# Thirty-two experts worked on in twelve units instead of thirteen

## The chip, the cores and the metric

One core of one Trainium2 chip runs the whole layer in one launch. The metric is device time in microseconds (us): 880.14 us before, the median of 3 runs (879.83 to 881.45). The engines are named as in the profile: PE (TensorE, with its weight loads as PEld), DVE (VectorE), ACT (ScalarE), POOL (GpSimd) and SP (SyncE, which issues all loads).

## The reference, cut to what matters

The layer mixes 512 tokens of width 1024 by pooling and attention, normalises, and then sends every token to 2 of 32 experts. An expert is three matrices of 2 MB each, so all experts together are 32 x 6 MB of weights that are read once from memory.

```python
group_probs = jax.nn.softmax(xf @ w_rg + b_rg, axis=-1)
g_idx = jnp.argmax(group_probs, axis=-1)                     # one of 4 groups
expert_logits = jnp.einsum('td,gde->tge', xf, w_re) + b_re   # 8 experts in a group
...
top_vals, top_idx = lax.top_k(sel_logits, TOP_K_IN_GROUP)    # two of the eight
...
for g in range(N_GROUPS):
    for e in range(EXPERTS_PER_GROUP):
        h = jax.nn.silu(xt @ w_eg[g, e]) * (xt @ w_eu[g, e])
        y = y + (h @ w_ed[g, e]) * combine[:, g, e, None]
...
ple = jax.nn.sigmoid(x @ w_pg[i]) * (p[i] @ w_pp[i])
x = layer_norm(DEEPNORM_ALPHA * x + moe_out + ple, ln2_g[i], ln2_b[i])
```

## The kernel before, in words

Up to about 370 us the kernel does the mixers, the first normalisation and the routing. From there on it works on the experts in **units**. A unit fills the 128 columns of PE with slots for tokens: a unit of kind `p` has two experts with 64 slots each, a unit of kind `q` four experts with 32 slots each. `KINDS = "ppppqqqpppppp"` lists the thirteen units 0 to 12. The first `FIXED` experts are taken by number, the others by rank, that is in order of how many tokens they got: the `BIG` largest get 64 slots (`CAP`), the rest 32. Ranks are known only when the counts are (`rank`), so until then only fixed experts can be loaded. If an expert had more tokens than slots, a branch at the end of the program would work on all experts again.

For each unit, `pair(j, ...)` does this on PE: `inner` (gate and up matrices, n = 0 and 1, eight k-steps each, all experts of the unit side by side as column parts of PE), the scatter of the unit before (`scatter_steps`), the turn of `h` (`hT_ps`), and `outer` (the down matrix, f = 0 to 3). In every second unit it also gathers the tokens of the next two units into slots (`gather`, 64 matmuls in two halves behind f = 1 and f = 3; a buffer `xg` for each unit, 2 of them). Before the change the odd units gather; the slots of units 0 and 1 are gathered during the routing. Units 3 to 6 (`EMB`) also carry the last term of the layer (`embedding`, `pg_ps`), in 26 steps.

Weights come in **pieces** of 1 MB (1.05 million bytes), 6 for each expert, 192 in all. SP issues them in one queue, in the order in which `load_chunk` is called. `eload_first` brings 18 pieces during the earlier stages; two of these lie in rooms (`acc`) that can't be used again, so 16 rooms circulate. `eload_past` runs behind every fourth k-step and every second f: it hands the rooms of the pieces just used to the next pieces. `KEEP` takes up to 8 rooms away from units 2 to 6 for the embedding; they come back at unit 7. In the last unit the last two pieces come as four halves, by columns.

The program's tail behind the last `outer` sums each block of tokens on PE, normalises and stores.

Of the kernel before, what the change touches and what calls it, by code (L numbers as in the profile page):

```python
# [21 lines left out]
NT = S // 128  # L22
# [4 lines left out]
LAG = 3  # L27


FIXED, BIG, CAP = 4, 16, 64  # L30
KINDS = "ppppqqqpppppp"
ALPHA = 2.0 ** 0.25
EPS = 1e-5

# [2 lines left out]
def layer_kernel(ctx: ExitStack, tc: tile.TileContext, x, p, w_in, w_pool, pool_scale, w_pu, w_au,  # L37
                 w_o, ln1_g, ln1_b, w_rg, b_rg, w_re, b_re, w_eg, w_eu, w_ed, w_pg, w_pp,
                 ln2_g, ln2_b, out):
    nc = tc.nc  # L40
# [37 lines left out]
    iota_c = cst.tile([128, CAP], F32, name="iota_c")  # L78
# [311 lines left out]
    units = [(h, tb) for h in range(HEADS) for tb in range(NT)]  # L390
    f = fill()
# [14 lines left out]
    for half in range(2):  # L406
        for br, (w, ah, al) in enumerate(((wpu, poh, pol), (wau, aoh, aol))):
            hi, lo = wnext()
            for c in range(4):
                g = gates[2 * br + half][:, c]  # L410
# [3 lines left out]
                o = mm()  # L414
# [17 lines left out]
    x1, acc = {}, {}  # L432
# [37 lines left out]
    units, chunk0, elist = [], [], []  # L470
    n_fixed, n_big, n_small = 0, 0, BIG
    for kind in KINDS:
        n = 2 if kind == "p" else 4
        if n_fixed < FIXED:
            who, n_fixed = (False, n_fixed), n_fixed + n
        elif n == 2:
            who, n_big = (True, n_big), n_big + n
        else:
            who, n_small = (True, n_small), n_small + n
        units.append(who + (n,))  # L480
        chunk0.append(len(elist))
        es = [(len(units) - 1, i) for i in range(n)]
        elist += [(w, e, slice(4 * kk, 4 * kk + 4), 4, FE) for w in (weg, weu) for kk in range(2) for e in es]
        elist += [(wed, e, slice(2 * kk, 2 * kk + 2), 2, D) for kk in range(2) for e in es]
    NU = len(units)
    assert n_fixed == FIXED and n_big == BIG and n_small == E - FIXED
    numbers = {}

    def expert(u, i):

        by_rank, first, _ = units[u]
        if not by_rank:
            return first + i
        if (u, i) not in numbers:
            r = first + i
            numbers[u, i] = nc.values_load(order[0:1, r:r + 1], engines=(mybir.EngineType.SP,), min_val=0, max_val=E - 1,
                                           skip_runtime_bounds_check_because="an expert's number")
        return numbers[u, i]

    def source(i):  # L500
# [2 lines left out]


    FIRST = [(0, "s8"), (1, "s8"), (2, "s8"), (4, "s8"), (5, "wraw"), (6, "whi"), (8, "wlo"), (9, "wraw"), (10, "s8"),
             (11, "s8"), (12, "s8"), (13, "s8"), (14, "whi"), (15, "wlo"), (3, "acc"), (16, "more"), (17, "more"),
             (7, "acc")]
    ew = {}

    room_of = {}  # L510

    def load_chunk(i, tag):
        room_of[i] = tag
        a, b = elist[i][3:]
# [20 lines left out]
    def eload_past(n):  # L535

        while done[0] < n:
            tag = room_of[done[0]]
            done[0] += 1
            if tag == "s8" and kept[0] < keep[0]:  # L540
                kept[0] += 1
            elif tag != "acc":
                free.append(tag)
        while free and len(ew) < len(elist):
            load_chunk(len(ew), free.pop(0))

    def give_back():

# [257 lines left out]
    xgs = {}  # L806

    def slots_and_weights(u):
        by_rank, first, n = units[u]
        return [t[:, :, first:first + n] for t in ((ranked[False], ranked[True]) if by_rank else (posm, comb))]  # L810

    def one_hots(G, m, b):

        for i in range(G.shape[2]):
            pos, _ = slots_and_weights(2 * m + i)
            n = pos.shape[2]
            shape = [128, 2, n, 128 // n]
            nc.vector.tensor_tensor(G[:, :, i].rearrange("p b (e c) -> p b e c", e=n),
                                    iota_c[:, None, None, :128 // n].to_broadcast(shape),
                                    pos[:, b:b + 2, :, None].to_broadcast(shape), op=OP.is_equal)  # L820

    def gather(G, o, kb, tbs):

# [13 lines left out]
        nc.tensor.matmul(o, strict[:, :1].to_broadcast([128, 128]), strict[:, None].to_broadcast([128, 4, 128]),  # L837
                         start=True, stop=False)

    def slots_of(m):  # L840
        for j in range(2 * m, min(2 * m + 2, NU)):
            xgs[j] = slp.tile([128, KD, 128], F32, name="xg", bufs=2)

    def keep_slots(m, o, kb):
        o = o.rearrange("p (k e s) -> p k e s", k=2, e=2)
        ks = slice(2 * kb, 2 * kb + 2)
        nc.scalar.activation(xgs[2 * m][:, ks], o[:, :, 0], AF.Copy)
        if 2 * m + 1 < NU:
            nc.vector.tensor_copy(xgs[2 * m + 1][:, ks], o[:, :, 1])

    def weights_of(j):

        pos, com = slots_and_weights(j)
        n = pos.shape[2]
        shape = [128, NT, n, 128 // n]

        if j < NU - 1:
            Gw = ex.tile([128, NT, 128], F32, name="Gw", tag="yh", bufs=2)
        else:
            Gw = outs[1][:, 0, :512].rearrange("p (b s) -> p b s", b=NT)  # L860
        G4 = Gw.rearrange("p b (e c) -> p b e c", e=n)
        nc.vector.tensor_tensor(G4, iota_c[:, None, None, :128 // n].to_broadcast(shape),
                                pos[:, :, :, None].to_broadcast(shape), op=OP.is_equal)
        nc.vector.tensor_mul(G4, G4, com[:, :, :, None].to_broadcast(shape))
# [19 lines left out]
    def inner(j, n, o, ks):  # L884


        ne = units[j][2]
        c = 128 // ne
        for k in ks:
            for i in range(ne):  # L890
                nc.tensor.matmul(o[i * c:(i + 1) * c], xgs[j][:, k, i * c:(i + 1) * c],  # L891
                                 ew[chunk0[j] + ne * (2 * n + k // 4) + i][:, k % 4], start=k == 0, stop=k == KD - 1)
            if k % 4 == 3:
                eload_past(chunk0[j] + ne * (2 * n + k // 4 + 1))

    with tc.manual_schedule():
        G = [lnt.tile([128, 2, 2, 128], F32R, name="G")]
        dve, pool = nc.vector, nc.gpsimd
        out_proj(0, 1, o, parts)
        eload_first(9)  # L900
# [50 lines left out]
        affine(2, 1, pool)  # L951
        normalise(3)
        place(0)
        one_hots(G[0], 0, 0)
        gain(2, 0, dve)
        xs = [mm("xg_ps") for _ in range(4)]
        for o in xs:
# [22 lines left out]
        eload_first(18)  # L980
        place(2)
        gather(G, xs[3], 3, (0, 1))
        G.append(lnt.tile([128, 2, 2, 128], F32R, name="G", tag="wr2"))
        one_hots(G[1], 0, 2)
        counted = count_tokens()
        slots_of(0)
        for kb in range(4):
            gather(G, xs[kb], kb, (2, 3))
            keep_slots(0, xs[kb], kb)
            if kb == 1:  # L990
                first = mm()
# [11 lines left out]
    def pair(j, other, extra):  # L1003


        last = j == NU - 1
        m = (j + 1) // 2 if j % 2 and j + 1 < NU else None

        def embed(i):
            for _ in range(extra[i]):  # L1010
# [2 lines left out]

        h = ex.tile([128, FE], F32, name="h", bufs=1)

        four = units[j][2] == 4

        def scatter():
            if other:
# [36 lines left out]
            scatter()  # L1056
            scatter()
        if m:
            G = [ex.tile([128, 2, min(2, NU - 2 * m), 128], F32R, name="G", tag="yl", bufs=2) for _ in range(2)]
            for b in range(2):  # L1060
                one_hots(G[b], m, 2 * b)
            slots_of(m)
# [17 lines left out]
        for f in range(4):  # L1080
            for c in range(2):
                outer(j, hT, f, c, o[c])
            if f % 2:
                eload_past(chunk0[j] + units[j][2] * (4 + (f + 1) // 2))
            if m and f % 2:
                og = [zz("xg_ps") for _ in range(2)]
                for i in range(2):
                    gather(G, og[i], f - 1 + i, range(NT))
                    keep_slots(m, og[i], f - 1 + i)
            if f == 1:  # L1090
                embed(4)
                Gt, ws = turn_one_hots(Gw)
# [1 line left out]
        return Gt, [weighted(o[c], ws) for c in range(2)]  # L1094

    def outer(j, hT, f, c, o):
        ne = units[j][2]
        n = 128 // ne
        for i in range(ne):
            nc.tensor.matmul(o[i * n:(i + 1) * n], hT[:, f, i * n:(i + 1) * n],  # L1100
                             ew[chunk0[j] + ne * (4 + f // 2) + i][:, f % 2, halves[c]], start=f == 0, stop=f == 3)

    def weighted(o, ws):
# [267 lines left out]
```

## Time and profile before

| what | value |
|---|---|
| median of 3 runs | 880.14 us |
| the profiled execution | 882.05 us, its span 880.3 us |
| PE busy | 824.1 us (94%) |
| DMA queue of the loads, share of 16 engines | 70.6% |
| mean granted TensorE clock | 0.972 |

The profile's span runs from the first instruction to the last; the execution's own time is 1.75 us longer. A busy PE counts overlapping matmuls once, so a share of 94% says that PE was rarely without work, not which resource set the pace.

### The profile page before, as it was taken

The numbers are of one execution on the slowest core, as the hardware profiler recorded it, in microseconds if no ns is written. First come the engines' busy times: TensorE is split into PE (matmuls) and PEld (weight loads), VectorE is DVE, ScalarE is ACT, GpSimd is POOL, SyncE is SP. The second block draws the span as 40 slices with busy tenths as digits, with TensorE's granted clock in tenths as the row PEclk, the third lists the DMA queues.
The fourth block names the chain that finished last, engine by engine and source line by source line (L and its number), as shares of the span: only waits on it lengthen the run. The fifth ranks groups of instructions, "written<-read, shape, count | busy, mean of one in ns | idle before, by whom it ended". The sixth has DMA issues, their size and how long they took to land.

```text
span 880.3 us, 11414 instructions
## 1 busy us (share of the span) xinstructions
PE 824.1 (94%) x4382; PEld 524.5 (60%) x4382; DVE 421.6 (48%) x705; ACT 216.8 (25%) x447; POOL 192.1 (22%) x176
## 2 busy tenths in 40 slices
PE   8999899899999998899999977989899999999993
PEld 7886677677768886734545522656765544644542
DVE  5278647554558758775244331222131424442347
ACT  3123444453551115212100211202010011010134
POOL 3333324233322227300002202211230000000045
PEclk9999999999999999699999989999999999999997
DMA  7431131312115796489999799999999999999962
GB/s 251 141 98 49 48 96 48 96 48 96 48 49 190 199 392 240 181 312 408 406 421 385 282 418 417 410 407 383 385 386 418 420 419 420 418 420 420 420 243 98
DMA packets 65786, 241.87 MB, mean 275 GB/s; under 512 B 12096, under 2 KB 32576, under 8 KB 41408
## 3 DMA queue, kind: packets, MB, share of 16 engines
q1 hardware_dynamic: 65728, 241.10, 70.6%
q8 instruction: 36, 0.59, 0.3%
q14 instruction: 22, 0.18, 0.1%
HBM read 238.99 MB, written 2.10 MB: 274 GB/s over the span
## 4 chain that ended last, share of the span: by engine, by line
PE 55%; DMA 9%; DVE 3%; POOL 2%; issue 1%; ACT 1%; SPq 1%; POOLq 0%; DVEq 0%; ACTq 0%
PE mm L891 18%; PE mm L1100 10%; PE xg_ps L830 6%; PE sc_ps L1133 5%; DMA ew<-in_w_ed_dram 4%; DMA ew<-in_w_eu_dram 3%; PE mm L142 3%; PE mm L144 3%; PE mm L143 3%; DMA ew<-in_w_eg_dram 2%; PE pg_ps L142 1%; PE pg_ps L143 1%; PE pg_ps L144 1%; PE hT_ps L1050 1%; PE gt_ps L870 1%
## 5 line engine op out<-in xcount | busy, mean ns | idle before, releaser
L891 PE MATMUL mm<-ew,xg 128*64 128x512 f32 (+1 forms) x1024 | 194.7, 605 | 10.7 <-DMA ew<-in_w_eu_dram 7.8
L891 PEld LDWEIGHTS mm<-ew,xg 128*64 128x64 f32 (+1 forms) x1024 | 60.5, 128 | 130.4 <-issue 109.0
L1100 PE MATMUL mm<-ew,hT 128*64 128x512 f32 (+1 forms) x512 | 100.5, 610 | 4.4 <-DMA ew<-in_w_ed_dram 3.4
L131 POOL TENSOR_TENSOR wlo<-wraw,whi 128x1024 fp32r<-128x1024 f32 x23 | 69.1, 3003 | 107.4 <-DVE whi L126 53.0
L142 PE MATMUL mm<-xth,whi 128*128 128x512 f32 x224 | 90.8, 406 | 0.0
L144 PE MATMUL mm<-xth,wlo 128*128 128x512 f32 x224 | 88.0, 393 | 0.0
L143 PE MATMUL mm<-xtl,whi 128*128 128x512 f32 x224 | 88.0, 393 | 0.0
L1037 DVE TENSOR_TENSOR h<-mm,h 128x512 f32<-128x512 f32 x26 | 18.0, 692 | 130.4 <-PE mm L891 71.8
L830 PEld LDWEIGHTS xg_ps<-G,x 128*128 128x128 f32 x448 | 57.6, 202 | 11.4 <-issue 7.4
L1100 PEld LDWEIGHTS mm<-ew,hT 128*64 128x64 f32 (+1 forms) x512 | 27.7, 127 | 60.6 <-issue 51.9
L1134 DVE TENSOR_TENSOR acc<-acc,sc_ps 128x512 f32<-128x512 f32 x96 | 59.6, 681 | 6.6 <-PE sc_ps L1133 6.0
L830 PE MATMUL xg_ps<-G,x 128*128 128x256 f32 (+1 forms) x448 | 61.0, 296 | 0.0
L144 PEld LDWEIGHTS mm<-xth,wlo 128*128 128x128 f32 x224 | 42.5, 190 | 9.3
L142 PEld LDWEIGHTS mm<-xth,whi 128*128 128x128 f32 x224 | 42.4, 189 | 9.5 <-issue 0.9
L143 PEld LDWEIGHTS mm<-xtl,whi 128*128 128x128 f32 x224 | 42.6, 190 | 8.4 <-issue 0.3
L1122 POOL TENSOR_TENSOR accl<-acc,acch 128x512 fp32r<-128x512 f32 x8 | 10.8, 1390 | 167.7 <-ACT acch L1121 167.7
L126 DVE CAST whi<-wraw 128x2048 fp32r<-128x2048 f32 x22 | 27.0, 1225 | 32.2 <-PE mm L143 15.0
L1133 PE MATMUL sc_ps<-yh,Gt 128*128 128x512 f32 x96 | 40.6, 423 | 1.1 <-DVE sg L1205 1.1
L131 DVE TENSOR_TENSOR wlo<-wraw,whi 128x1024 fp32r<-128x1024 f32 x23 | 40.7, 1769 | 1.0
L143 PE MATMUL pg_ps<-pgl,xT 128*128 128x256 f32 x128 | 36.9, 289 | 3.0 <-POOL pgl L1185 3.0
L1205 DVE TENSOR_TENSOR sg<-pg_ps,sg 128x256 f32<-128x256 f32 x16 | 6.8, 425 | 68.3 <-ACT sg L1204 68.3
L1133 PE MATMUL sc_ps<-yl,Gt 128*128 128x512 f32 x96 | 37.9, 395 | 0.0
(270 smaller groups left out, 1342.2 us busy)
## 6 DMA issues: line engine op xcount, KB each, us to landing
ew<-in_w_eg_dram SPq DMA_DIRECT2D x64, 1024.0 KB, 11.4
ew<-in_w_eu_dram SPq DMA_DIRECT2D x64, 1024.0 KB, 11.8
ew<-in_w_ed_dram SPq DMA_DIRECT2D x62, 1024.0 KB, 14.1
wraw<-in_w_in_dram SPq DMA_DIRECT2D x15, 1024.0 KB, 5.6
wraw<-in_w_o_dram SPq DMA_DIRECT2D x4, 1024.0 KB, 4.9
pgr<-in_w_pg_dram SPq DMA_DIRECT2D x4, 1024.0 KB, 14.7
wraw<-in_w_pu_dram SPq DMA_DIRECT2D x2, 1024.0 KB, 5.1
wraw<-in_w_au_dram SPq DMA_DIRECT2D x2, 1024.0 KB, 4.9
```

The costliest lines, as they stand in the source:

```text
L126: nc.vector.tensor_copy(hi, wraw[i])
L131: eng.tensor_sub(lo[:, j], wraw[i][:, j], hi[:, j].bitcast(F32))
L142: nc.tensor.matmul(o, lh, rh, start=start, stop=False)
L143: nc.tensor.matmul(o, lh, rl, start=False, stop=False)
L144: nc.tensor.matmul(o, ll, rh, start=False, stop=stop)
L830: nc.tensor.matmul(o[:, kx * 256:kx * 256 + n], x1[tb][:, i, cs], G[tb // 2][:, tb % 2].rearrange("p u s -> p (u s)"), start=whole and tb ...
L891: nc.tensor.matmul(o[i * c:(i + 1) * c], xgs[j][:, k, i * c:(i + 1) * c], ew[chunk0[j] + ne * (2 * n + k // 4) + i][:, k % 4], start=k == ...
L1037: nc.vector.tensor_mul(ht, o, ht)
L1100: nc.tensor.matmul(o[i * n:(i + 1) * n], hT[:, f, i * n:(i + 1) * n], ew[chunk0[j] + ne * (4 + f // 2) + i][:, f % 2, halves[c]], start=f ...
L1122: nc.gpsimd.tensor_sub(l, acc[tb][:, halves[c]], h.bitcast(F32))
L1133: nc.tensor.matmul(o, Gt[:, tb * 128:(tb + 1) * 128], y[c][i], start=i == 0, stop=i == 1)
L1134: nc.vector.tensor_add(acc[tb][:, cs], acc[tb][:, cs], o)
```

## The change

`FIXED` becomes 3, `BIG` 13, and a third kind of unit, `m`, holds three experts: one with 64 slots and two with 32. Sixteen experts have 64 slots now (before twenty), sixteen have 32 (before twelve). The order of units is `p m p p q q q p p p p m`. In an `m` unit the 64 slots are two column parts of 32 that use the same weights, so `inner` and `outer` run four column parts as in a `q` unit. Only unit 0 is gathered during the routing (128 slots instead of 256 for each matmul); the even units now gather for the next two units, unit 0 for 1 and 2, unit 10 for 11 alone. The 18 pieces of `FIRST` are again those of fixed experts: all twelve of unit 0, and the six of expert 2 in unit 1; `sequence` puts the others behind them in their order.

```diff
-FIXED, BIG, CAP = 4, 16, 64
-KINDS = "ppppqqqpppppp"
+FIXED, BIG, CAP = 3, 13, 64
+KINDS = ("pm" "pp" "qqq" "pppp" "m")
...
+        n64, n32 = {"p": (2, 0), "m": (1, 2), "q": (0, 4)}[kind]
...
+    n_experts, columns = [], []
+    for groups in units:
+        caps = [cap for _, _, n, cap in groups for _ in range(n)]
+        w = min(caps)
+        n_experts.append(len(caps))
+        who = [i for i, cap in enumerate(caps) for _ in range(cap // w)]
+        columns.append([(i, slice(w * c, w * c + w)) for c, i in enumerate(who)])
...
-             (11, "s8"), (12, "s8"), (13, "s8"), (14, "whi"), (15, "wlo"), (3, "acc"), (16, "more"), (17, "more"),
+             (11, "s8"), (12, "s8"), (15, "s8"), (18, "whi"), (21, "wlo"), (3, "acc"), (24, "more"), (27, "more"),
              (7, "acc")]
+    sequence = [i for i, _ in FIRST] + [i for i in range(len(elist)) if i not in dict(FIRST)]
...
-            load_chunk(len(ew), free.pop(0))
+            load_chunk(sequence[len(ew)], free.pop(0))
...
-            for i in range(ne):
-                nc.tensor.matmul(o[i * c:(i + 1) * c], xgs[j][:, k, i * c:(i + 1) * c],
+            for i, cs in columns[j]:
+                nc.tensor.matmul(o[cs], xgs[j][:, k, cs],
                                  ew[chunk0[j] + ne * (2 * n + k // 4) + i][:, k % 4], start=k == 0, stop=k == KD - 1)
...
-        G = [lnt.tile([128, 2, 2, 128], F32R, name="G")]
+        G = [lnt.tile([128, 2, 1, 128], F32R, name="G")]
...
-        m = (j + 1) // 2 if j % 2 and j + 1 < NU else None
+        m = range(j + 1, min(j + 3, NU)) if j % 2 == 0 else None
...
-    KEEP = {(2, 5): 2, (3, 3): 4, (3, 5): 5, (4, 0): 6, (4, 1): 7, (4, 2): 8}
+    KEEP = {(2, 5): 2, (3, 1): 4, (3, 5): 5, (4, 0): 6, (4, 1): 7, (4, 2): 8}
```

The first place is PE at the end of unit 0. Before, `inner` of unit 0 (L891, two column parts of 64), the turn of `h`, `outer` (L1100) in two halves with the turn of the weights (`gt_ps`) between them, and then `inner` of unit 1 follow each other:

```order
L891 MATMUL mm<-ew,xg 64x512 x24
L1050 MATMUL hT_ps<-ident,h 128x128 x4
L1100 MATMUL mm<-ew,hT 64x512 x8
L870 MATMUL gt_ps<-ident,Gw 128x128 x4
L1100 MATMUL mm<-ew,hT 64x512 x8
L891 MATMUL mm<-ew,xg 64x512 x32
L1133 MATMUL sc_ps<-yh,Gt 128x512
```

Now the same engine at the same place (the lines have moved: 891 is 907, 1050 is 1066, 1100 is 1115, 830 is 848):

```order
L907 MATMUL mm<-ew,xg 64x512 x24
L1066 MATMUL hT_ps<-ident,h 128x128 x4
L1115 MATMUL mm<-ew,hT 64x512 x8
L848 MATMUL xg_ps<-G,x_2688 128x256 x2
L848 MATMUL xg_ps<-G,x_2742 128x256 x2
L848 MATMUL xg_ps<-G,x_2924 128x256 x2
L848 MATMUL xg_ps<-G,x_2927 128x256 x2
```

And the end of that gather, where unit 1, now of kind `m`, begins:

```order
L848 MATMUL xg_ps<-G,x_2688 128x256 x2
L848 MATMUL xg_ps<-G,x_2742 128x256 x2
L848 MATMUL xg_ps<-G,x_2924 128x256 x2
L848 MATMUL xg_ps<-G,x_2927 128x256 x2
L907 MATMUL mm<-ew,xg 32x512 x64
L1148 MATMUL sc_ps<-yh,Gt 128x512
```

The gather for units 1 and 2 has moved into unit 0, one half ahead of the second half of `outer` and one behind it, so 64 matmuls now stand between the first rooms that `outer` gives back and unit 1; unit 1 has twice as many matmuls of half the columns.

The second place is SP's queue, at the end of `eload_first` and where the loads by rank begin (`TENSOR_LOAD order` reads an expert's number). Before:

```order
L521 DMA ew<-in_w_ed_dram 128x2048 x4
L521 DMA ew<-in_w_eg_dram 128x2048 x5
L521 DMA ew<-in_w_eu_dram 128x2048 x5
L521 DMA ew<-in_w_ed_dram 128x2048 x4
L496 TENSOR_LOAD order
L521 ISA
L521 DMA ew<-in_w_eg_dram 128x2048
```

Now:

```order
L536 DMA ew<-in_w_ed_dram 128x2048 x4
L536 DMA ew<-in_w_eg_dram 128x2048 x2
L536 DMA ew<-in_w_eu_dram 128x2048 x2
L536 DMA ew<-in_w_eg_dram 128x2048
L536 DMA ew<-in_w_ed_dram 128x2048 x2
L536 DMA ew<-in_w_eu_dram 128x2048
L510 TENSOR_LOAD order
L536 ISA
L536 DMA ew<-in_w_eg_dram 128x2048
```

Six of the pieces that stood ahead of the first number are now loaded by rank: the numbers are wanted from the 19th piece on, before from the 25th.

## Rows read from the trace of the kernel before

**Rows 1.** Windows at the starts of units 0 to 7, and the tail: busy by engine.

```profile
core 0: us, PE busy (x) PEld busy (x) DVE busy (x) ACT busy (x) POOL busy (x), PEclk, DMA share, GB/s
370.70:397.00 26.30, 24.75 (x121) 9.41 (x122) 17.97 (x39) 5.24 (x9) 0.00 (x0) 1.00 0.74 275
397.00:430.70 33.70, 33.70 (x186) 17.93 (x182) 15.33 (x26) 4.90 (x9) 0.00 (x0) 1.00 1.00 412
430.70:456.70 26.00, 26.00 (x124) 10.54 (x124) 10.61 (x17) 3.37 (x6) 0.00 (x0) 1.00 1.00 410
456.70:490.30 33.60, 33.60 (x186) 17.88 (x182) 12.79 (x23) 3.10 (x7) 4.76 (x2) 1.00 0.87 346
490.30:536.80 46.50, 38.60 (x256) 14.43 (x256) 16.89 (x27) 10.38 (x17) 10.47 (x4) 0.90 0.98 391
536.80:611.40 74.60, 68.82 (x526) 46.13 (x520) 16.50 (x31) 9.12 (x17) 11.69 (x10) 1.00 1.00 401
611.40:675.60 64.20, 59.59 (x457) 40.14 (x456) 13.69 (x24) 10.07 (x16) 16.74 (x11) 0.97 0.98 396
675.60:711.70 36.10, 34.86 (x186) 18.59 (x184) 13.18 (x24) 3.89 (x8) 0.73 (x1) 1.00 1.01 419
...
849.80:880.30 30.50, 15.15 (x68) 8.18 (x66) 18.59 (x34) 13.02 (x27) 17.37 (x16) 0.81 0.21 75
```

**Rows 2.** The chain that ended last, in order of time: start us, us, what.

```profile
673.70 14.53 DMA ew<-in_w_eu_dram
688.27 3.65 PE mm L891 x14
```

**Rows 3.** Timeline of SP's issues: start us, us, line, tensors, how many.

```profile
393.07 5.08 SPq L521 DMA_DIRECT2D ew<-in_w_eg_dram  x4
400.68 4.35 SPq L521 DMA_DIRECT2D ew<-in_w_eu_dram  x4
...
470.59 0.39 SPq L1154 DMA_DIRECT2D pr<-in_p_dram  x1
486.47 8.97 SPq L521 DMA_DIRECT2D ew<-in_w_eu_dram  x5
```

**Rows 4.** Windows from 478 to 516 us, columns as in rows 1.

```profile
478.00:492.00 14.00, 14.00 (x104) 9.63 (x104) 4.22 (x9) 2.70 (x6) 0.00 (x0) 1.00 0.68 246
492.00:500.00 8.00, 8.00 (x69) 3.39 (x62) 3.33 (x6) 1.37 (x3) 4.73 (x2) 1.00 0.79 289
...
508.00:512.00 4.00, 0.00 (x0) 0.00 (x0) 0.77 (x2) 0.00 (x0) 0.00 (x0) 0.78 1.00 416
512.00:516.00 4.00, 3.80 (x20) 0.99 (x24) 0.00 (x0) 0.00 (x0) 0.00 (x0) 0.50 1.02 424
```

**Rows 5.** Timeline of PE at five places: start us, us, line, tensors, shape, how many.

```profile
366.31 3.76 PE L830 MATMUL xg_ps<-G,x 128*128 128x256 f32 x16
...
389.39 3.65 PE L1100 MATMUL mm<-ew,hT 128*64 128x512 f32 x16 [0.69 <-ACT hT L1052]
...
603.90 3.64 PE L1100 MATMUL mm<-ew,hT 128*32 128x512 f32 x32
607.47 4.01 PE L830 MATMUL xg_ps<-G,x 128*128 128x256 f32 x32
...
819.58 3.79 PE L830 MATMUL xg_ps<-G,x 128*128 128x128 f32 x32
```

**Rows 6.** Loads by line: from 390 to 396 us, and the last four halves.

```profile
DMA to landing us min/median/max: 5.2/6.5/7.8
...
L526 SPq DMA_DIRECT2D ew<-in_w_ed_dram x4: 373/384/2804, 825.6 to 833.0; - x4
...
DMA to landing us min/median/max: 16.8/18.6/20.2
```

**Rows 7.** Timeline: DVE in unit 0, PE in the last unit.

```profile
389.22 9.21 DVE L882 TENSOR_TENSOR acc<-x 128x1024 f32<-128x1024 f32 x4
...
850.41 7.09 PE L1100 MATMUL mm<-ew,hT 128*64 128x512 f32 x32 [0.25 <-ACT hT L1052]
```

More of the change, by code (lines that the diff above doesn't have):

```diff
@@ L472, in layer_kernel @@
     for kind in KINDS:
[L473 to L480, printed above, removed]
+        n64, n32 = {"p": (2, 0), "m": (1, 2), "q": (0, 4)}[kind]
+        groups = []
+        n = min(n64, FIXED - n_fixed)
+        if n:
+            groups.append((False, n_fixed, n, CAP))
+            n_fixed += n
+        if n64 - n:
+            groups.append((True, n_big, n64 - n, CAP))
+            n_big += n64 - n
+        if n32:
+            groups.append((True, n_small, n32, CAP // 2))
+            n_small += n32
+        units.append(groups)
         chunk0.append(len(elist))
-        es = [(len(units) - 1, i) for i in range(n)]
+        es = [(len(units) - 1, i) for i in range(n64 + n32)]
         elist += [(w, e, slice(4 * kk, 4 * kk + 4), 4, FE) for w in (weg, weu) for kk in range(2) for e in es]
@@ L486, in layer_kernel @@
     assert n_fixed == FIXED and n_big == BIG and n_small == E - FIXED
+    n_experts, columns = [], []
[5 more added lines that the diff above has]
+        columns.append([(i, slice(w * c, w * c + w)) for c, i in enumerate(who)])
     numbers = {}
     def expert(u, i):
-        by_rank, first, _ = units[u]
+        by_rank, r = [(g[0], g[1] + k) for g in units[u] for k in range(g[2])][i]
         if not by_rank:
-            return first + i
+            return r
         if (u, i) not in numbers:
-            r = first + i
             numbers[u, i] = nc.values_load(order[0:1, r:r + 1], engines=(mybir.EngineType.SP,), min_val=0, max_val=E - 1,
@@ L808, in slots_and_weights, with one_hots @@
     def slots_and_weights(u):
[L809 to L820, printed above, removed]
+        c = 0
+        for by_rank, first, n, cap in units[u]:
+            yield [t[:, :, first:first + n] for t in ((ranked[False], ranked[True]) if by_rank else (posm, comb))] + [
+                n, cap, slice(c, c + n * cap)]
+            c += n * cap
+    def one_hots(G, us, b):
+        for i, u in enumerate(us):
+            for pos, _, n, cap, cs in slots_and_weights(u):
+                shape = [128, 2, n, cap]
+                nc.vector.tensor_tensor(G[:, :, i, cs].rearrange("p b (e c) -> p b e c", e=n),
+                                        iota_c[:, None, None, :cap].to_broadcast(shape),
+                                        pos[:, b:b + 2, :, None].to_broadcast(shape), op=OP.is_equal)
     def gather(G, o, kb, tbs):
@@ L838, in open_bank, with slots_of, keep_slots @@
                          start=True, stop=False)
-    def slots_of(m):
-        for j in range(2 * m, min(2 * m + 2, NU)):
+    def slots_of(us):
+        for j in us:
             xgs[j] = slp.tile([128, KD, 128], F32, name="xg", bufs=2)
-    def keep_slots(m, o, kb):
+    def keep_slots(us, o, kb):
         o = o.rearrange("p (k e s) -> p k e s", k=2, e=2)
         ks = slice(2 * kb, 2 * kb + 2)
-        nc.scalar.activation(xgs[2 * m][:, ks], o[:, :, 0], AF.Copy)
-        if 2 * m + 1 < NU:
-            nc.vector.tensor_copy(xgs[2 * m + 1][:, ks], o[:, :, 1])
+        nc.scalar.activation(xgs[us[0]][:, ks], o[:, :, 0], AF.Copy)
+        if len(us) > 1:
+            nc.vector.tensor_copy(xgs[us[1]][:, ks], o[:, :, 1])
     def weights_of(j):
-        pos, com = slots_and_weights(j)
-        n = pos.shape[2]
-        shape = [128, NT, n, 128 // n]
         if j < NU - 1:
@@ L860, in weights_of @@
             Gw = outs[1][:, 0, :512].rearrange("p (b s) -> p b s", b=NT)
[L861 to L864, printed above, removed]
+        for pos, com, n, cap, cs in slots_and_weights(j):
+            shape = [128, NT, n, cap]
+            G4 = Gw[:, :, cs].rearrange("p b (e c) -> p b e c", e=n)
+            nc.vector.tensor_tensor(G4, iota_c[:, None, None, :cap].to_broadcast(shape),
+                                    pos[:, :, :, None].to_broadcast(shape), op=OP.is_equal)
+            nc.vector.tensor_mul(G4, G4, com[:, :, :, None].to_broadcast(shape))
         return Gw
@@ L884, in inner @@
     def inner(j, n, o, ks):
-        ne = units[j][2]
-        c = 128 // ne
+        ne = n_experts[j]
         for k in ks:
-            for i in range(ne):
-                nc.tensor.matmul(o[i * c:(i + 1) * c], xgs[j][:, k, i * c:(i + 1) * c],
+            for i, cs in columns[j]:
+                nc.tensor.matmul(o[cs], xgs[j][:, k, cs],
                                  ew[chunk0[j] + ne * (2 * n + k // 4) + i][:, k % 4], start=k == 0, stop=k == KD - 1)
@@ L953, in layer_kernel @@
         place(0)
-        one_hots(G[0], 0, 0)
+        one_hots(G[0], (0,), 0)
         gain(2, 0, dve)
@@ L982, in layer_kernel @@
         gather(G, xs[3], 3, (0, 1))
-        G.append(lnt.tile([128, 2, 2, 128], F32R, name="G", tag="wr2"))
-        one_hots(G[1], 0, 2)
+        G.append(lnt.tile([128, 2, 1, 128], F32R, name="G", tag="wr2"))
+        one_hots(G[1], (0,), 2)
         counted = count_tokens()
-        slots_of(0)
+        slots_of((0,))
         for kb in range(4):
             gather(G, xs[kb], kb, (2, 3))
-            keep_slots(0, xs[kb], kb)
+            keep_slots((0,), xs[kb], kb)
             if kb == 1:
@@ L1014, in pair @@
         h = ex.tile([128, FE], F32, name="h", bufs=1)
-        four = units[j][2] == 4
+        four = n_experts[j] == 4
         def scatter():
@@ L1058, in pair @@
         if m:
-            G = [ex.tile([128, 2, min(2, NU - 2 * m), 128], F32R, name="G", tag="yl", bufs=2) for _ in range(2)]
+            G = [ex.tile([128, 2, len(m), 128], F32R, name="G", tag="yl", bufs=2) for _ in range(2)]
             for b in range(2):
@@ L1083, in pair @@
             if f % 2:
-                eload_past(chunk0[j] + units[j][2] * (4 + (f + 1) // 2))
+                eload_past(chunk0[j] + n_experts[j] * (4 + (f + 1) // 2))
             if m and f % 2:
@@ L1096, in outer @@
     def outer(j, hT, f, c, o):
[L1097 to L1100, printed above, removed]
+        ne = n_experts[j]
+        for i, cs in columns[j]:
+            nc.tensor.matmul(o[cs], hT[:, f, cs],
                              ew[chunk0[j] + ne * (4 + f // 2) + i][:, f % 2, halves[c]], start=f == 0, stop=f == 3)
```

## The prediction

> **What bounds the kernel now.** I read the windows by unit first [rows 1]. In units 1 to 3 PE is busy for the whole stretch, in 4 to 6 it is not, and in the tail it is busy half the time. So far this looks like a kernel bound by PE, in which a unit less is worth a unit's length. The last two columns tell another story: from unit 1 on the loads run at 412 and 410 GB/s, fall to 346 in unit 3, come back to 391, 401 and 396, and stand at 419 in unit 7. At 419 GB/s a piece (1.0486 MB) takes 2.50 us, so the two experts of a `p` unit take 30.0 us. On PE a `p` unit takes 26.0 us without a gather (unit 2) and 33.7 with one (unit 1), 29.9 on average. PE and queue are level, within a tenth of a microsecond.
>
> The chain [rows 2] shows who leads whom: the last time that PE waits for a piece ends at 688.27, after a load of 14.53 us; from there to the end it is PE's own work. The queue is hardly behind it: the last half piece is issued at 833.0 and lands 16.8 us later [rows 6], at 849.8, and the last unit's `outer` begins at 850.4 [rows 7]. Shortening PE's work alone moves the end by next to nothing beyond that point; then the last landing sets the time. The question is when the queue can be done.
>
> Where does the queue lose time against 419 GB/s? In 478 to 492 it runs at 246 and to 500 at 289 [rows 4]: 14 x (1 - 246/419) + 8 x (1 - 289/419) = 5.8 + 2.5 = 8.3 us. The cause stands in SP's issues [rows 3]: after 470.6 nothing is issued until 486.5. Every room is full or kept for the embedding, and PE has not used enough pieces. Units 5 and 6 lose 74.6 x (1 - 401/419) + 64.2 x (1 - 396/419) = 3.2 + 3.5 = 6.7 us, beside the embedding's own loads.
>
> **The change part by part.**
>
> *A unit less on PE.* One `p` unit without a gather goes: 26.0 us. The number of gathers in units stays six (before in 1, 3, ... 11; now in 0, 2, ... 10). An `m` unit costs what a `p` unit costs: 16 matmuls with 64 columns took 3.65 us, 32 with 32 columns 3.64 [rows 5], so four parts side by side take no longer than two, and I take nothing for it. The extra small one-hot operations of DVE for `m` fall in units where DVE is busy for 10.6 of 26.0 us [rows 1]; cover gone, they would cost under a microsecond each.
>
> *The pieces stay 192.* They can't come faster than 2.50 us each. Here the Trainium skill speaks against any gain at all: its page "DMA: Bandwidth & Descriptors", section Specifications, limits a core to about 358 GB/s from memory, by which (an estimate) the 177 MB after piece 29 would take 494 us and the kernel would end near 934. The row of unit 7, 419 GB/s, disagrees, and the row decides.
>
> *The gather in unit 0.* Two halves of 4.01 us [rows 5] now stand ahead of unit 1, so it starts at 397.0 + 8.0. The second half needs the banks that ACT and DVE empty behind the renewal of `acc` on DVE, which ends at 389.22 + 9.21 = 398.4 [rows 7]; six one-hots now stand ahead of it. I allow 0.6 us of waiting (bounds 0 and 3): unit 1 starts at 405.6. What is queued behind on DVE is unit 0's own `Gt` and `yl`, needed only in unit 1's scatter.
>
> *What that does to the queue.* Unit 0 gives back ten rooms (two of its twelve are `acc`), for pieces 19 to 28. Piece 29 needs a room of unit 1, which is free after four k-steps, 3.65 us: at 409.3. Landing takes 5.2 us from an idle queue [rows 6], so piece 29 lands at 414.5. Before, piece 25 was issued at 393.07, landed at 398.3, and four more at 2.55 us (412 GB/s) put piece 29 at 408.5. **Loss: 6.0 us.**
>
> *What it gives back.* From there units 1 to 3 use 18 + 12 + 12 pieces instead of 36. Unit 3 ends at 405.6 + 26.0 + 33.7 + 26.0 = 491.3, within a microsecond of before, with 54 pieces used instead of 48. Six pieces more used and 2.4 fewer brought make 8.4 rooms, 21 us of loading, where the queue stood still for 16. The hole at 478 to 500 should close: **gain 8.3 us.** The numbers by rank are now wanted from the 19th piece on, which was issued after DVE had them; I take nothing for it.
>
> *The last landing.* 849.8 + 6.0 - 8.3 = 847.5. PE must be ready by then. Counting back 66 pieces of 2.50 us, unit 6 has its last piece at about 682.5; half an `outer`, half a gather and one step of the embedding (some 4.4 us, from the busy time of unit 5 less 33.7, over eight) take it to 694.5. Four units take 119.4 us and the last unit's part ahead of `outer` 18.9 (26.0 less 7.1): 833. That is 12 us early, so the tail waits for loads, not for PE.
>
> *The tail.* Before, the whole `outer` (7.09 us) stood behind the last landing. Now it follows the halves: those of the first columns land 2.5 us ahead of the last, and six of eight steps, 5.3 us, remain, so `outer` ends 2.8 us behind the last landing, at 850.3. From its end (857.5) to the end of the span took 22.8 us and is not touched: **873.1 us**.
>
> *Bounds that I put at nothing.* The routing's gather goes from 256 columns to 128. At the full clock 32 matmuls took 4.01 and 3.79 us, nearly the same; 16 at the lower one took 3.76 [rows 5]. If half the columns help there, 24 matmuls save up to 2.4 us; against that, after a wait the last `outer` can run at half clock, up to 5.3 us. I let the two cancel.
>
> The profiled execution took 882.05, its span 880.3, and the median of the runs is 880.14, so I take the span less 0.2: **873 us**.
>
> **The rivals.**
>
> *Full value of a unit:* 880.3 - 26.0 = 854. Against it speak the bytes: piece 29 at 414.5 and 163 pieces and 5.8 MB of embedding loads behind it at 2.50 us end no sooner than 836, and 25.6 us later it is 861.5. It takes an earlier piece 29. Chance 0.03.
>
> *The queue runs without a hole:* with the backlog carried into units 5 and 6, their 6.7 us go too, and the routing's 2.4: 864. For it, a queue that is behind has issues waiting; against it, the embedding still keeps 8 rooms. Chance 0.20.
>
> *The hole only moves:* with 8 rooms left, units 4 and 6 now carry a gather beside the embedding, PE uses four pieces at a time, and the 8.3 us are lost there instead: 881, no change. Chance 0.12.
>
> *Slower, by the clock:* after the empty stretch 508 to 512 the next 4 us ran at 0.50 [rows 4], 1.2 GHz. If PE now waits at every group of four pieces in units 4 to 6, where before it lost 46.5 - 38.6 + 74.6 - 68.8 + 64.2 - 59.6 = 18.3 us, and each wait is followed by as much work at half clock, its work there (167 us and a gather, 8) grows past what the 24 x 3 pieces and the embedding's loads take (78 x 2.55 = 199). It decides from some 24 us of lost PE time on; at 32 us it costs 8 there, and 5 more in the last `outer`: 886. [...] Chance 0.12.
>
> *The capacity fails:* only 16 experts may have over 32 tokens now. In the reference's own draw the largest of the small half has exactly 32, so the branch at the end is not taken; were it, 192 pieces more at 2.50 us would make it 1350. Chance 0.01.
>
> **How the numbers follow.** The forecast has 0.52, within 868 to 877. Faster by over 0.2% (below 878.4; 0.2% is about what the runs can tell from no change): 0.52 + 0.20 + 0.03 and a quarter of the moved hole, 0.78. Same: 0.09. Slower: 0.13. The range that leaves out 2 in 10 is 863 to 881: from the queue without a hole to the hole that only moves.
>
> **What would show it.** Right: GB/s stays above 400 from about 414 on, through the old hole; PE waits for `ew` in the last two units; the last half lands near 847 and `outer` ends within 4 us of it. Wrong: SP standing still again for over 5 us in units 3 to 6; a landing of piece 29 far from 414; PE without waits in the last units, which would mean PE still leads; or a granted clock of 0.50 in more than a few stretches.

## The result and the profile after

The changed kernel takes 873.91 us (873.22 to 874.19, 4 runs) against 880.48 us (879.83 to 881.45, 4 runs) on the same chip: a ratio of 0.9922, with a 95% interval of 0.991 to 0.9934. It is faster by 6.6 us, and 0.9 us behind the forecast of 873. The profiled execution took 873.73 us, its span 871.9 us. The one profiled before took 882.05, its span 880.3: it lies above all four runs, so the spans differ by 8.4 us where the times differ by 6.6.

First the windows of the changed kernel at the starts of its units 0 to 7, the last unit up to the last landing, and the tail. They answer to [rows 1]; the columns are the same.

```profile
core 0: us, PE busy (x) PEld busy (x) DVE busy (x) ACT busy (x) POOL busy (x), PEclk, DMA share, GB/s
371.80:409.50 37.70, 34.91 (x189) 17.70 (x190) 22.70 (x47) 7.36 (x13) 0.00 (x0) 0.94 0.70 262
409.50:435.40 25.90, 25.90 (x217) 9.62 (x216) 10.81 (x19) 3.38 (x6) 0.00 (x0) 1.00 0.89 360
435.40:469.20 33.80, 33.80 (x190) 18.00 (x186) 12.80 (x23) 3.08 (x7) 0.00 (x0) 1.00 1.01 419
469.20:495.20 26.00, 26.00 (x122) 10.35 (x121) 10.64 (x17) 3.42 (x6) 4.69 (x2) 1.00 1.01 420
495.20:554.70 59.50, 46.76 (x322) 23.00 (x320) 19.26 (x33) 8.47 (x16) 4.73 (x2) 0.91 1.02 413
554.70:618.70 64.00, 59.48 (x458) 38.45 (x458) 14.21 (x25) 12.75 (x19) 19.61 (x13) 1.00 1.02 411
618.70:694.60 75.90, 69.66 (x526) 46.26 (x520) 16.41 (x31) 9.11 (x17) 14.56 (x11) 0.98 1.01 406
694.60:720.50 25.90, 25.90 (x121) 10.50 (x122) 10.62 (x17) 3.30 (x6) 0.73 (x1) 1.00 1.01 419
...
813.90:846.50 32.60, 29.17 (x203) 10.31 (x206) 13.50 (x18) 8.12 (x15) 10.48 (x8) 0.95 1.01 408
846.50:871.90 25.40, 10.34 (x54) 6.38 (x46) 16.78 (x30) 9.68 (x21) 12.39 (x12) 0.79 0.28 102
```

Read the last column downwards. Unit 0 is 11.4 us longer than before and brings pieces no faster; unit 1 runs at 360 GB/s, where it ran at 412 before; from unit 2 on the queue runs at 406 to 420 GB/s to the last landing. The dip to 346 in unit 3 and the 391 of unit 4 in [rows 1] are gone. PE now waits for loads at the end: it is idle for 3.4 of 32.6 us in the last unit, where before it had waited 0.25 [rows 7].

The longest pieces of the chain that ended last in the changed kernel, from the start of its last unit to the end of `outer` (start us, us, what), answer to [rows 2]:

```profile
814.00 7.03 PE mm L907 x64
821.03 10.02 DMA ew<-in_w_eu_dram
831.09 4.25 PE mm L907 x23
835.35 8.43 DMA ew<-in_w_ed_dram
843.82 5.34 PE mm L1115 x42
```

Before, PE's own work made up the chain from 688 us to the end of `outer`. Now loads stand in it until 843.8.

SP's issues in the changed kernel where the hole was (start us, us, line, tensors, how many), beside [rows 3]:

```profile
454.79 7.81 SPq L536 DMA_DIRECT2D ew<-in_w_ed_dram  x4
464.76 17.79 SPq L536 DMA_DIRECT2D ew<-in_w_eg_dram  x8
484.66 0.39 SPq L1169 DMA_DIRECT2D pr<-in_p_dram  x1
491.12 8.88 SPq L536 DMA_DIRECT2D ew<-in_w_eu_dram  x6
```

Issues go on up to 485, where SP had stood still for 16 us before, and the same 14 us in which the loads ran at 246 GB/s [rows 4] now show 420:

```profile
478.00:492.00 14.00, 14.00 (x66) 6.42 (x64) 7.11 (x12) 0.60 (x1) 4.69 (x2) 1.00 1.01 420
```

SP does stand still again, from 485.1 to 491.1 and for up to 11 us at a time in units 4 to 6. I had named over 5 us of that as a sign of being wrong. It was a bad sign: the pieces already issued kept the queue at 406 GB/s and more in each of these units. One sign of being right came only by half: PE waits for `ew` in the last unit, but not in the one before it.

The last half piece, from the loads by line of the changed kernel, is issued at 836.5 and lands 9.9 us later, at 846.5:

```profile
L541 SPq DMA_DIRECT2D ew<-in_w_ed_dram x2: 373/373/373, 836.0 to 836.5; - x2
...
DMA to landing us min/median/max: 9.2/9.6/9.9
```

### The profile page after: what moved, and what is told of

Read it like the earlier page. It is cut to its first block, busy times and chain, and to the rows that moved or that the text cites. A ratio compares the mean times of both kernels' runs of the same rounds, so it can differ in the third digit from the quotient of the medians.

```text
span 871.9 us, 11544 instructions
## 1 busy us (share of the span) xinstructions
PE 805.8 (92%) x4454; PEld 511.5 (59%) x4454; DVE 412.3 (47%) x691; ACT 214.2 (25%) x443; POOL 191.4 (22%) x176
## 4 chain that ended last, share of the span: by engine, by line
PE 50%; DMA 11%; DVE 4%; POOL 2%; issue 1%; ACT 1%; SPq 1%; POOLq 0%; ACTq 0%; DVEq 0%
PE mm L907 18%; PE mm L1115 8%; PE xg_ps L848 6%; DMA ew<-in_w_eu_dram 4%; PE sc_ps L1148 4%; PE mm L143 3%; PE mm L145 3%; PE mm L144 3%; DMA ew<-in_w_ed_dram 3%; DMA pr<-in_p_dram 2%; DMA ew<-in_w_eg_dram 2%; PE pg_ps L144 1%; PE pg_ps L143 1%; PE pg_ps L145 1%; DVE acc L899 1%
## 5 line engine op out<-in xcount | busy, mean ns | idle before, releaser
L907 PE MATMUL mm<-ew,xg 128*32 128x512 f32 (+1 forms) x1088 | 189.5, 621 | 16.8 <-DMA ew<-in_w_eu_dram 11.1
L907 PEld LDWEIGHTS mm<-ew,xg 128*32 128x32 f32 (+1 forms) x1088 | 54.8, 125 | 137.3 <-issue 108.3
L1115 PE MATMUL mm<-ew,hT 128*32 128x512 f32 (+1 forms) x544 | 91.6, 597 | 3.0 <-DMA ew<-in_w_ed_dram 2.1
L848 PE MATMUL xg_ps<-G,x 128*128 128x256 f32 (+1 forms) x448 | 59.0, 290 | 1.2 <-DVE xg L867 1.2
L1149 DVE TENSOR_TENSOR acc<-acc,sc_ps 128x512 f32<-128x512 f32 x88 | 54.7, 681 | 6.6 <-PE sc_ps L1148 6.0
L1115 PEld LDWEIGHTS mm<-ew,hT 128*32 128x32 f32 (+1 forms) x544 | 24.7, 120 | 54.5 <-issue 46.1
L1164 POOL TENSOR_TENSOR xf<-x 128x1024 f32<-128x1024 f32 x4 | 9.4, 2376 | 144.5 <-PE mm L907 144.5
L1148 PE MATMUL sc_ps<-yh,Gt 128*128 128x512 f32 x88 | 37.8, 429 | 1.1 <-DVE sg L1220 1.1
```

What stands on the lines that cost most here:

```text
L848: nc.tensor.matmul(o[:, kx * 256:kx * 256 + n], x1[tb][:, i, cs], G[tb // 2][:, tb % 2].rearrange("p u s -> p (u s)"), start=whole and tb ...
L907: nc.tensor.matmul(o[cs], xgs[j][:, k, cs], ew[chunk0[j] + ne * (2 * n + k // 4) + i][:, k % 4], start=k == 0, stop=k == KD - 1)
L1115: nc.tensor.matmul(o[cs], hT[:, f, cs], ew[chunk0[j] + ne * (4 + f // 2) + i][:, f % 2, halves[c]], start=f == 0, stop=f == 3)
L1148: nc.tensor.matmul(o, Gt[:, tb * 128:(tb + 1) * 128], y[c][i], start=i == 0, stop=i == 1)
L1149: nc.vector.tensor_add(acc[tb][:, cs], acc[tb][:, cs], o)
```

## The experiments

They ask four things: whether PE or the queue sets the end of each kernel, what SP's last standstill does, whether the tail hangs on the last halves, and what the gather in unit 0 and the place of the unit of three are worth. Each ran beside the kernel before on one chip; its median there was 880.67 for the first four, 880.92 for the next four and, on another chip, 879.96 for the last two. A ratio is always to that kernel before. The five edits of the changed kernel that keep its units act from unit 8 on or later, and yet their traces run 0.5 to 2.6 us ahead of its own at the start of unit 7. The cause of that stays open. So these five are also counted from there to the end of the span: 871.9 - 694.6 = 177.3 us in the changed kernel, whose unit 7 begins here (PE's timeline, as in the two like it below):

```profile
694.61 1.94 PE L907 MATMUL mm<-ew,xg 128*64 128x512 f32 x8
```

**More work for PE, before and after.** `warm`, a helper of the kernel, runs matmuls of the identity, which depend on nothing.

```diff
         h = ex.tile([128, FE], F32, name="h", bufs=1)
+        if j == 8:
+            warm(48)
```

In the kernel before:

> The kernel before, with 48 more matmuls of 128 columns on PE at the start of unit 8 (no data of the layer is touched); at about 0.11 us each that is 5.5 us. Theory (before, PE leads from 688 us on; after, the queue of loads leads): the kernel before gets slower by the whole 5.5 us, to about 886. Rival (the queue leads in the kernel before too): no change, 880.5.

In the changed kernel:

> The changed kernel with the same 48 matmuls at the start of unit 8, some 5.5 us of PE. Theory (the queue leads behind unit 6, PE has some 9 us to spare in the last units): no change, 873.9, and PE's waits for loads in the last unit shrink by about 5 us. Rival (PE leads, and the gain is a unit's work less its new waits): slower by 5.5 us, 879.4.

The dose was twice what I thought. This is PE's timeline of the changed kernel with the added work: 48 matmuls stand as 96, and take 10.98 us.

```profile
718.92 10.98 PE L151 MATMUL warm_ps<-ident 128*128 128x128 f32 x96
```

The kernel before took 890.91 us (ratio 1.0101, 1.008 to 1.0121): 10.2 of 11 us came through by the medians, 8.9 by the ratio, as they should where PE leads. The changed kernel took 882.65 (ratio 1.0021, 1.001 to 1.0032), 8.7 us more than without them. In its trace unit 7 begins 1.7 us earlier, and from there to the end of the span it takes 881.2 - 692.9 = 188.3 us, 11.0 more: all of the added work.

```profile
692.91 1.51 PE L907 MATMUL mm<-ew,xg 128*64 128x512 f32 x6
```

That is against my theory, which had 9 us to spare for PE (12 in the prediction). Windows of this kernel show what happened:

```profile
816.00:820.00 4.00, 4.00 (x25) 1.76 (x21) 0.84 (x2) 0.00 (x0) 0.00 (x0) 1.00 0.38 154
820.00:824.00 4.00, 4.00 (x38) 3.10 (x40) 0.15 (x1) 1.52 (x4) 0.00 (x0) 1.00 0.00 0
824.00:828.00 4.00, 4.00 (x44) 1.24 (x40) 1.26 (x2) 0.40 (x1) 0.00 (x0) 1.00 0.15 29
828.00:832.00 4.00, 4.00 (x32) 1.90 (x28) 1.36 (x3) 0.84 (x3) 0.00 (x0) 1.00 0.97 377
```

The queue ran dry. From unit 10 on the program keeps eight rooms back for the tail (`keep[0] = 8` at `NU - 2`), and the last unit now has 18 pieces where it had 12. So SP has no room after 801 until unit 11 itself gives some back, 3.6 us after its start. In the changed kernel as it is, that is just soon enough: the piece issued at 801.0 lands 19.8 us later, at 820.8, the next is issued at 817.6 and lands 5.7 us later, at 823.3, one piece's time behind. These are its loads by line, of the window around that issue:

```profile
L536 SPq DMA_DIRECT2D ew<-in_w_eu_dram x1: 332/332/332, 817.6 to 817.6; - x1
...
DMA to landing us min/median/max: 5.7/5.7/5.7
```

With the added work, the same issue of that kernel comes at 826.4:

```profile
L536 SPq DMA_DIRECT2D ew<-in_w_eu_dram x1: 333/333/333, 826.4 to 826.4; - x1
...
DMA to landing us min/median/max: 5.0/5.0/5.0
```

It lands at 831.4, 12.4 us behind the one before it (799.2 + 19.8 = 819.0), so 9.9 us of loading are lost. A landing takes 5.0 us here and took 5.7 where there was no hole: by these two, 0.7 us is all the cover that PE's work ahead of unit 11 has. I formed the theory anew: whatever delays unit 11 delays the last landings, through the rooms.

**Fewer bytes, before and after.** The four gate pieces of unit 8 are loaded by half, 5.0 us of loading less; `inner` uses that half twice, so the other half of these gate matrices is left out of the result.

```diff
-            nc.sync.dma_start(ew[i], source(i))
+            nk = 2 if elist[i][0] is weg and elist[i][1][0] == 8 else a
+            nc.sync.dma_start(ew[i][:, :nk], source(i)[:, :nk])
```

In the kernel before:

> The kernel before, in which unit 8 loads only half of each of its four gate pieces (2.1 MB less; it computes with the half that is there, so its output is not the layer's). At 419 GB/s that is 5.0 us of the queue. Theory: PE leads behind 688 us, so no change or at most 1 us, 880. Rival (the queue leads): 5 us faster, 875.5.

In the changed kernel:

> The changed kernel with the same half pieces in unit 8 (2.1 MB less, output not the layer's). Theory (the queue leads to the end): the last landing comes 5.0 us sooner and the kernel is 5 us faster, 869; PE's waits in the last unit shrink by as much. Rival (PE leads): no change, 873.9.

The kernel before took 879.96 us (ratio 0.9979, 0.9966 to 0.9992): 0.7 us less by the medians, 1.8 by the ratio, though its last half landed 6.3 us earlier, at 843.5. The changed kernel took 871.11 (ratio 0.9888, 0.9869 to 0.9907), 2.8 us less than without the edit. The trace does not put these down to the bytes. Unit 7 begins 2.6 us earlier, ahead of the edit, and from there to the end of the span it takes 869.4 - 692.0 = 177.4 us, as without the edit: that is the rival's 0. The 5.0 us went into the same standstill.

```profile
692.05 1.51 PE L908 MATMUL mm<-ew,xg 128*64 128x512 f32 x6
```

Windows of the changed kernel with fewer bytes:

```profile
809.00:813.00 4.00, 4.00 (x41) 2.43 (x44) 1.11 (x2) 1.93 (x4) 0.00 (x0) 1.00 0.68 283
813.00:817.00 4.00, 4.00 (x44) 1.27 (x40) 0.30 (x1) 0.00 (x0) 0.00 (x0) 1.00 0.37 88
```

The pieces come earlier, but the rooms do not: 4 x (1 - 283/419) + 4 x (1 - 88/419) = 4.5 us of loading are lost at 809 to 817. So the changed kernel's end hangs on two things that happen to be level, its queue and the start of unit 11: a queue with less to bring gains nothing while unit 11 starts no sooner.

**Five rooms kept instead of eight.** If that coupling is what made the 11 us cost so much, three rooms more should take most of it away, and without the added work they should bring nothing.

```diff
-                keep[0] = 8
+                keep[0] = 5
...
-            assert kept[0] >= 7
+            assert kept[0] >= 5
```

With the 48 matmuls:

> The changed kernel with the same 48 matmuls more in unit 8, but only five rooms kept for the tail from unit 10 on instead of eight, so that SP can issue three pieces more before it stands still. Theory (the 8.7 us that the 48 matmuls cost came through the rooms: they made unit 11 start later, SP had no room before, and the queue ran empty for 9.8 us): three pieces are 7.5 us of loading, 2.3 us of the hole remain, the last landing is near 849 and the time 874 to 877. Rival (any PE time counts once, whatever the queue does): 882 to 883, as with eight kept.

Without them:

> The changed kernel with five rooms kept for the tail instead of eight, and nothing else. Theory (without the added matmuls the landings follow each other every 2.5 us through SP's standstill, so earlier issues bring nothing): 873.9, within 0.5. Rival (the standstill of SP from 801 to 818 costs time by itself): 870 to 872.

With them it took 876.07 us (ratio 0.9943, 0.993 to 0.9957), 6.6 us less than with eight rooms kept and the same work on PE; the rival had 882 to 883. From the start of unit 7 (692.8) to the end of the span it takes 180.5 us, so 3.2 of the 11 us remain. What is left of the hole in its windows:

```profile
816.00:820.00 4.00, 4.00 (x25) 1.76 (x21) 0.78 (x2) 0.00 (x0) 0.00 (x0) 1.00 1.02 420
820.00:824.00 4.00, 4.00 (x38) 3.03 (x41) 0.22 (x1) 1.59 (x4) 0.00 (x0) 1.00 1.00 414
824.00:828.00 4.00, 4.00 (x44) 1.30 (x40) 1.19 (x2) 0.33 (x1) 0.00 (x0) 1.00 0.40 125
```

Without them it took 872.75 (ratio 0.9904, 0.9889 to 0.9919), 1.2 us below the changed kernel where I expected 0.5 at most; the intervals overlap, and its early units alone ran about a microsecond ahead of those of the changed kernel (unit 1 began at 408.5 rather than 409.5). From the start of unit 7 (693.5) to the end of the span it takes 177.3 us, as the changed kernel does: rooms given back sooner, with the same bytes to bring, gain nothing either. The standstill of SP costs nothing by itself here, as long as nothing else is late.

**The last two pieces whole.**

```diff
-        if i < len(elist) - 2:
+        if i < len(elist):
             nc.sync.dma_start(ew[i], source(i))
```

> The changed kernel with its last two pieces loaded whole instead of in halves of columns. Theory (the tail hangs on the last landing, and the halves let the first columns go 2.5 us ahead): the last piece still lands near 846.5, but the first columns wait for it too, so six of the eight steps of the last products stand behind it where there were four: 876 to 877. Rival (PE itself sets the end): no change, 873.9.

It took 877.14 us (ratio 0.9954, 0.994 to 0.9968), 3.2 us more. PE's timeline in this kernel shows the same 42 matmuls that stood at 843.82 in the changed kernel, now behind the last whole piece:

```profile
844.27 1.04 PE L1115 MATMUL mm<-ew,hT 128*32 128x512 f32 x2 [1.44 <-DMA ew<-in_w_ed_dram]
846.81 5.34 PE L1115 MATMUL mm<-ew,hT 128*32 128x512 f32 x42 [1.49 <-DMA ew<-in_w_ed_dram]
```

The end moved by 846.81 - 843.82 = 3.0 us: the tail hangs on the landing of the last pieces, and on which columns come first.

**Four fixed experts.** Twelve units again, but unit 1 is a pair of fixed experts, so that the routing gathers for units 0 and 1 as it did before the change, and unit 0 gathers nothing. The odd units gather, and one gather fewer stands in the units (five).

```diff
-FIXED, BIG, CAP = 3, 13, 64
-KINDS = ("pm" "pp" "qqq" "pppp" "m")
+FIXED, BIG, CAP = 4, 12, 64
+KINDS = ("pp" "mp" "qqq" "pppp" "m")
...
-        m = range(j + 1, min(j + 3, NU)) if j % 2 == 0 else None
+        m = range(j + 1, min(j + 3, NU)) if j % 2 and j + 1 < NU else None
```

(`FIRST`, the routing's one-hots and the place of one entry of `KEEP`, `(3, 3)` for `(3, 1)`, are those of the kernel before.)

> Twelve units as in the change, but with four experts fixed and 12 with 64 slots, so that unit 1 is a pair of fixed experts, the routing gathers for units 0 and 1 (256 columns) and no gather stands in unit 0; the unit of three is the third. One gather in a unit fewer. Theory (the gather in unit 0 makes unit 1 start 8 to 9 us late, and with it the 29th piece and every landing behind it, the last one too): unit 1 starts near 397, piece 29 lands near 409, the last landing near 838, the time 864 to 867. Rival (the queue stands still again in units 3 and 4, as before the change, because PE has not used enough pieces): the 8.3 us are lost there, 872 to 874.

It took 866.24 us (ratio 0.9824, 0.9811 to 0.9838), 7.7 us less than the changed kernel. Its windows at units 0 to 4:

```profile
370.70:397.10 26.40, 24.85 (x121) 9.43 (x122) 18.01 (x39) 5.04 (x9) 0.00 (x0) 1.00 0.73 273
397.10:430.80 33.70, 33.70 (x186) 17.90 (x182) 15.76 (x28) 5.11 (x9) 0.00 (x0) 1.00 1.01 415
430.80:456.80 26.00, 26.00 (x219) 9.68 (x218) 10.81 (x19) 3.42 (x6) 0.00 (x0) 1.00 1.00 406
456.80:490.50 33.70, 33.70 (x188) 17.97 (x184) 12.79 (x23) 3.04 (x7) 4.68 (x2) 1.00 1.01 418
490.50:541.20 50.70, 38.02 (x257) 15.76 (x258) 16.98 (x27) 10.49 (x17) 4.71 (x2) 0.93 1.02 412
```

Unit 1 begins at 397.1, as before the change, the loads are above 400 GB/s from there on, and there is no hole. Its last half piece, from the loads by line, is issued at 830.2 and lands 9.9 us later, at 840.1; the span ends 25.5 us behind that.

**The unit of three put late.** The same kernel with one edit:

```diff
-KINDS = ("pp" "mp" "qqq" "pppp" "m")
+KINDS = ("pp" "pp" "qqq" "mppp" "m")
```

> The kernel with four fixed experts (866.2 us) with its unit of three as the eighth unit instead of the third: units 0 to 3 are four pairs again, as in the kernel before, and by the end of unit 3 PE has used 48 pieces instead of 54. Still twelve units. Theory (the hole at 478 to 500 was closed by the six more pieces that PE uses up to there, not by the order of the loads or the experts' split): SP stands still again after 471, the loads fall below 360 GB/s in unit 3, some 8 us of loading are lost, the last landing goes from 840 to about 848 and the time to 872 to 875. Rival (the hole went for another reason): 866 to 867.

It took 875.08 us (ratio 0.9946, 0.9931 to 0.996), 8.8 us more by the medians, just above what the theory gave. The two kernels ran on different chips: by the ratios the difference is 10.7 us, and in the two traces, counted from the start of unit 0, it is (873.0 - 369.3) - (865.6 - 370.7) = 8.8. Its windows at units 3 and 4:

```profile
455.30:489.00 33.70, 33.70 (x186) 17.91 (x182) 12.79 (x23) 3.18 (x7) 4.75 (x2) 1.00 0.87 347
489.00:532.90 43.90, 36.58 (x257) 14.18 (x258) 16.90 (x27) 10.37 (x17) 10.43 (x4) 0.96 0.97 388
```

And SP's issues in it:

```profile
466.97 0.86 SPq L536 DMA_DIRECT2D ew<-in_w_eu_dram  x2
469.28 0.39 SPq L1169 DMA_DIRECT2D pr<-in_p_dram  x1
485.16 8.97 SPq L536 DMA_DIRECT2D ew<-in_w_eu_dram  x5
```

The hole of the kernel before is back almost to the digit: 347 and 388 GB/s for its 346 and 391 [rows 1], a standstill up to 485.2 for its 486.5 [rows 3]. Twelve units alone do not close it; six pieces more used by the end of unit 3 do.

**Three pieces in halves.** With four fixed experts and five rooms kept:

```diff
-        if i < len(elist) - 2:
+        if i < len(elist) - 3:
...
-                for j in (i - 1, i):
+                for j in (i - 2, i - 1, i):
```

> The kernel with four fixed experts, five rooms kept for the tail, and the last three pieces loaded in halves of columns instead of two: all three first halves, then all three second ones. Theory (the tail hangs on the last halves, and SP's standstill costs nothing where the landings follow each other): the last half of the first columns lands some 1.2 us earlier, and the time falls by 0.5 to 1.5 us, to 865 to 866. Rival (the order of the last halves does not count): 866.2.

It took 865.38 us (ratio 0.9836, 0.9821 to 0.9851). The median lies where the theory put it, but the two ratios, 0.9836 and 0.9824, don't differ by what their intervals can tell. The run also changes two things at once, the halves and the rooms, and most of its trace's lead stands already at the start of unit 7 (679.9 rather than 681.9). It stays open whether the third piece's halves count. The kernel with four fixed experts, at 866 us, is the fastest version that I can call faster than both.

## Why the prediction came out

The forecast was 873 and the time is 873.9, and its mechanism held: a unit's 26 us on PE brought little by itself, because the queue was level with PE, and the gain came from the hole and the tail less what the gather in unit 0 cost. Two of its terms were mis-sized in opposite directions, one of its covers was not there, and the step from span to time was off. That it came so close is in part luck.

- **A unit less on PE, by itself:** the kernel with the unit of three put late shows it apart, with twelve units, the hole as before and no gather in unit 0. It is 4.9 us faster than the kernel before beside it, and its span ends 25.5 us behind its last landing (issued at 834.7, 12.8 us, at 847.5) instead of 30.5. So what a unit less on PE brought by itself is no more than the tail's 5 us.
- **A unit of three costs what a pair costs:** right. Unit 1, 25.9 us with 128 matmuls in its two `inner`, where the pair in unit 3 takes 26.0.
- **The loss by the gather in unit 0: predicted 6.0, measured 8.9.** Unit 1 began at 409.5 instead of 405.6, and piece 29, which waits for its fourth k-step, was issued at 413.1 and landed 5.1 us later, at 418.2; before, it landed at 409.3.

```profile
L536 SPq DMA_DIRECT2D ew<-in_w_ed_dram x1: 333/333/333, 413.1 to 413.1; - x1
...
DMA to landing us min/median/max: 5.1/5.1/5.1
```

  In the five traces with the same unit 0 it landed at 415.9 to 417.8, so 8.9 is the upper end of a loss of 6.6 to 8.9. Unit 1 began 3.9 us later than forecast, and PE's timeline of the changed kernel shows where they are:

```profile
371.86 3.68 PE L907 MATMUL mm<-ew,xg 128*64 128x512 f32 x8
375.47 1.65 PE L848 MATMUL xg_ps<-G,x 128*128 128x128 f32 x8
377.04 1.94 PE L907 MATMUL mm<-ew,xg 128*64 128x512 f32 x8
...
392.66 3.65 PE L1115 MATMUL mm<-ew,hT 128*64 128x512 f32 x16 [0.69 <-ACT hT L1068]
396.24 4.00 PE L848 MATMUL xg_ps<-G,x 128*128 128x256 f32 x32
...
405.50 4.03 PE L848 MATMUL xg_ps<-G,x 128*128 128x256 f32 x32 [1.23 <-DVE xg L867]
```

  The wait for the second half is 1.23 us, 0.6 more than I allowed. The other 3.3 lie ahead: `outer` began at 392.66, before at 389.39 [rows 5]. The term that I had let cancel, the routing's gather with half the columns, came out as a loss. PE finished that gather sooner and then stood idle for DVE's routing for 5.72 us instead of 2.37; the granted clock stayed at 0.50 (1.2 GHz) from 363.9 to 375.5, and the first eight matmuls of unit 0 took 3.68 us instead of 1.94. With four fixed experts and 256 columns the clock is 1.00 from 371.8 on, and `outer` begins at 389.46.
- **The hole closed: right, and shown.** It closes with the pieces used early and comes back without them, 8.8 us in time by the medians (10.7 by the ratios) for the 8.3 predicted.
- **What the queue gained: predicted 8.3, measured 11.3.** By the arithmetic of the prediction, units 3 to 6 before lost 5.9 + 3.1 + 3.2 + 3.5 = 15.7 us against 419 GB/s; units 2 to 6 now lose 0.9 + 1.2 + 2.4 = 4.4. Units 3 and 4 alone, where the hole was, gained 8.1. The further 3 are a part of the rival in which the queue runs without any hole. Why units 5 and 6 run closer to 419 I have not tested.
- **The last landing:** 849.8 + 8.9 - 11.3 = 847.4, measured 846.5 (issued at 836.5, 9.9 us), predicted 847.5. The two errors in size cancel to 0.1, and that they do is luck.
- **The tail:** predicted 25.6 us behind the last landing, measured 25.4, of 30.5 before. The last two pieces whole cost 3.2 of these 5.1: it is the halves that let `outer` run ahead.
- **From the span to the time:** I had taken the span less 0.2, from a profiled execution that lay 1.9 us above its median. After the change the span is 871.9, 1.2 us less than the 873.1 forecast, and the median is the span plus 2.0. The two misses have opposite signs, so the time came within 0.9.
- **PE "12 us early": the step that failed.** It was right that the tail waits for loads, with `outer` beginning at 839.3, 7.2 us ahead of the last landing, though I had it at 833. But I took the 12 us as cover, and for work ahead of unit 11 there is 0.7. I had not followed the eight rooms kept from unit 10 on to SP's last issues: a late unit 11 is a late last landing. The forecast escaped because unit 7 began at 694.6, and I had said 694.5.

Of the rivals, a unit's full value and the moved hole did not come. The clock did not tip either: the granted clock in units 4 to 6 was 0.91, 1.00 and 0.98, for 0.90, 1.00 and 0.97 before. PE lost 12.7 + 4.5 + 6.2 = 23.5 us there, close to the 24 from which the rival would have decided, but that says little: it is what 175.9 us of work leave of the 199.4 us that the queue took.

## What to carry to other kernels

Here an engine and a load queue were level, and removing work from the engine paid only where it freed room for loads earlier or took work from behind the last landing; so in such a kernel reckon the order in which buffers come free, not the work saved. Before you call an engine early, ask which buffers its progress releases and whether the queue has anything left to issue without them: slack at the engine can be none at the queue. And look for the place at which the queue stands still: here six pieces used earlier were worth more than 8 us, as much as an 8 us gather put in front of unit 1's first release cost.

## What I had not expected of the hardware

Half the columns did not make the routing's gather faster where the clock was low: 16 matmuls with 128 columns took 3.65 us at a granted clock of 0.50, and 16 with 256 columns 3.76 us [rows 5] at 0.50 too. Where 24 of them with 128 columns ran at 1.00 they took 2.87 us, and the time saved turned into idle time and a longer stretch at the lower clock. A matmul of the identity, f32 in the trace, stands there as two, 0.11 us each (48 as 96 in 10.98 us), which doubled a dose that I had reckoned as one.
